# A ninth pair of quadrant products in a two-layer transformer block's second feed-forward

## The chip, the cores and the metric

The kernel runs on one core of one Trainium2 chip. The core has a matrix engine (TensorE, PE in the profile; its weight loads are PEld), a vector engine (VectorE, DVE), an activation engine (ScalarE, ACT), a general engine (GpSimd, POOL), a queue that issues transfers (SyncE, SP) and 16 DMA engines. The engines run their own instruction streams in order and meet at semaphores. Working memory is the SBUF of 128 partitions; TensorE writes to PSUM. The metric is the device time of one execution in microseconds (us), as the median of several runs.

## The reference, cut to what matters

One sequence of 512 tokens and 1024 features runs through two layers, in float32. Each layer mixes (spatial gating in the first, forgetting attention in the second, memory attention in both) and then runs a gated feed-forward of width 2816:

```python
f = rmsnorm(h, ln_ffn_pre[layer])
f = (jax.nn.silu(f @ w_ffn_gate[layer]) * (f @ w_ffn_up[layer])) @ w_ffn_down[layer]
h = h + rmsnorm(f, ln_ffn_post[layer])
```

The change is in the feed-forward of the second layer, whose output is the kernel's output.

## The kernel before, in words

**Numbers in two parts.** Each float32 operand is split into a high part (a cast on ScalarE, L276) and a low part (a subtraction on VectorE, L277). A product of two operands is three products on TensorE: high by high, high by low, low by high (`mm3`, L219 to L221). The split parts of a weight block, 128x512 each, go into `pair_of_parts` (L125), a ring of eight pairs.

**Row tiles.** The hidden width of 2816 is 22 row tiles of 128 rows, 0 to 21. For each row tile, gate and up are matrix products of weight blocks with the normed input; then the hidden value is silu(gate) times up. Row tiles 0 and 1 are computed plainly at the boundary from the mixing stage. The others come in pairs (2 and 3, 4 and 5, to 20 and 21).

**Seven products for eight.** For a pair of row tiles and the two halves of the input, `Seven` (L1098) takes a two-by-two block product with seven quadrant products in place of eight. `run(n)` does quadrant n: 12 products of 128x256 on TensorE, then evacuations on ScalarE and a sum on VectorE (L1150 to L1170). After the seventh (`run(3)`) the rows are handed on: `gate_rows` (L1309) applies the row scale and silu, `up_rows` (L1315) multiplies gate and up. A set (`sets(m)`, L1327) is one `Seven` for gate and one for up, for row tiles m and m+1; the last quadrant of each is run after the first two quadrants of the next, where there is a next.

**Down, in quadrants and plainly.** The down product of most pairs also goes by seven quadrant products (`Down`, L1174): the two row tiles by the two halves of the tokens and of the output. Its operands are sums of hidden values, formed on VectorE (`sums`, `last_sum`) and split (`form`); its weights are loaded and summed (`weights`), some sums by transfers that add in DRAM (`sums_ahead`, L170). A quadrant is six products of 128x512. One quadrant runs during the sets (`straight`, L1333). The other six wait until all sets are done: a first pass takes quadrants 0, 3, 6 and 5 of each pair, a second pass quadrants 1 and 4. Before the change `ones = 8` pairs go this way, row tiles 2 to 17.

**The tail.** The remaining row tiles, 18 to 21, are computed by two further sets after the passes; `up_rows` splits their hidden values at once (`some`). Their down product is done plainly in the tail (`tail_of`, L877), token tile by token tile (four of 128 tokens): for each of the two output halves, three products per row tile, so 24 products of 128x512 for a token tile; the last token tile's second half is done in two pieces of 256 columns. Then VectorE adds the product to the sum so far (L904), ScalarE squares it (L917), VectorE and GpSimd form the normalisation factor (L924, L290), and ScalarE scales the two halves (L944). `give` (L1708) turns them back on TensorE (L955), adds them to the residual on VectorE (L960) and sends them out; it does so for a token tile while the next one's products run. The last token tile has a variant of its own (L905 to L940, `give_last`).

**Places.** While the sets run, the residual rows are parked in DRAM and their tile, `room`, holds four places for weights of 128x1024; `more_raws` (L1298) hands them out in a circle: to the first gate set, to the up set's two loads from row tile 4 on, and in the passes to the weights of every second pair. `places` (L1303) makes a `Down` with its three tiles for hidden values and sums.

The order of the work on each engine comes from the code's order and a scheduler that may move an instruction ahead of others that wait; each engine then runs its stream in the order given.

Of the kernel before, what the change touches and what calls it, by code (L numbers as in the profile page):

```python
# [8 lines left out]
F32 = mybir.dt.float32  # L9
# [34 lines left out]
def hybrid(ctx: ExitStack, tc: tile.TileContext, i: dict, out: bass.AP):  # L44
# [14 lines left out]
    def name(s):  # L59
        n_of[s] = n_of.get(s, 0) + 1  # L60
        return f"{s}_{n_of[s]}"

    def act(s, dt=F32R, shape=(P, T)):
        return ap.tile(list(shape), dt, tag="a", name=name(s))

    def plain(s, shape=(P, T), dt=F32):
        return yp.tile(list(shape), dt, tag="y", name=name(s))
# [7 lines left out]
    def small(s, n=4, dt=F32):  # L75
        return sp.tile([P, n], dt, tag=f"s{n}", name=name(s))
# [131 lines left out]
    def down_weights(layer, k, dh, aside=False):  # L208
        return moving_pair(i["w_down"][layer, 4 * dh : 4 * dh + 4, :, k : k + 2, :]
                           .rearrange("m p k c -> p m (k c)"), aside)  # L210
# [145 lines left out]
    def rows_tile(s, dt=F32):  # L356
        return hp.tile([P, KT, T], dt, tag="h", name=name(s))
# [886 lines left out]
    def feed_forward(layer, phase, xp, meanwhile=None):  # L1244
        nonlocal h
        nnorm = PairNorm()
        rb = rbc
        ones = 8

        def hidden(gate, up, f, cols):  # L1250
            c0, c1 = cols
# [9 lines left out]
        fs = [(act("fhi"), act("flo")) for _ in range(2)]  # L1261
# [9 lines left out]
        a, close = boundary(phase, G_MIX_POST + layer, G_FFN_PRE + layer, nnorm, rb, first, evac_first, scaled)  # L1271
# [9 lines left out]
        xs, last = combined(a, scaled, xp)  # L1281
        last()
        ys = [[None] * 2 for _ in range(TB)]
# [9 lines left out]
                nc.sync.dma_start(kept_y[tb, dh], y)  # L1293

        room = rows_tile("room")
        places_of_raws = cycle([room[:, 2 * n : 2 * n + 2, :].rearrange("p a b -> p (a b)") for n in range(4)])

        def more_raws():  # L1298
            return next(places_of_raws)

        downs, gates = [], {}

        def places():  # L1303
            j = len(downs)
            downs.append(Down(layer, 2 + 2 * j, act("u", F32), plain("u"),
                              act("t", F32) if j < 4 else plain("t")))
            return downs[j].u0, downs[j].u1

        def gate_rows(row, g):  # L1309
# [16 lines left out]

        def sets(m, some=None):  # L1327
            sums_ahead()
            yield Seven(xs, "w_gate", layer, m, "mm", gate_rows, raws=more_raws if m == 4 else None)
            yield Seven(xs, "w_up", layer, m, "lg", lambda row, u: up_rows(row, u, some), None if some else places,  # L1330
                        more_raws if m > 2 else None)

# [32 lines left out]
        one, two, aside = [], [], []  # L1365
# [54 lines left out]
        for j, d in enumerate(downs):  # L1420
# [5 lines left out]
            if 0 < j < 7:  # L1426
                tb, dh, some = late[j - 1]
# [5 lines left out]
                    V.tensor_add(y, y, some)  # L1433
                    ys[tb][dh] = y

        fs = [(act("fhi"), act("flo")) for _ in range(4)]
        before = None
        for m in (18, 20):
            if meanwhile and m == 20:
                next(meanwhile)  # L1440
            for n, u in enumerate(sets(m, fs[m - 18 : m - 16])):
                u.run(1)
                u.run(7)
                if before:
                    before.run(3)
                for x in (6, 4, 5, 2) if n and m == 20 and not layer else (6, 4, 2, 5):
                    u.run(x)
                before = u
# [7 lines left out]
        eps = small("eps")  # L1456
        V.tensor_mul(eps, nnorm.r4, nnorm.r4)
        V.reciprocal(eps, eps)
        V.tensor_scalar_mul(eps, eps, RMS_EPS)
        return tail_of(fs, lambda kp, dh, aside: down_weights(layer, 18 + 2 * kp, dh, aside), ys, eps, layer == 1, True)  # L1460


    def layer_b(phase, fp):
# [237 lines left out]
    with tc.tile_pool(name="ffn0", bufs=4) as xp:  # L1701
        phase = feed_forward(0, phase, xp, memory())
    with tc.tile_pool(name="fox", bufs=1) as fp:
        phase = layer_b(phase, fp)
    with tc.tile_pool(name="ffn1", bufs=4) as xp:
        tail, ys, _ = feed_forward(1, phase, xp, end_gains())
# [102 lines left out]
```

## Time and profile before

| What | Value |
|---|---|
| Runs before: median, lowest, highest (3 runs) | 1083.52, 1082.90, 1083.83 us |
| Profiled execution: span | 1081.0 us |
| Runs' median less the span (what lies around it) | 2.5 us |
| TensorE busy | 1073.2 us, 99% of the span |
| VectorE busy | 942.9 us, 87% |
| ScalarE busy | 736.4 us, 68% |
| DMA, mean over the span | 166 GB/s |

The profile page gives no other time for the profiled execution than its span, from the first to the last instruction; what a run takes beyond it is the third row. In the views, a time is in us from the span's start. The chain of waits goes back from the last instruction, at each step to what released it. A group of instructions has a line, an engine, an operation, the names written and read with shapes, a count, the busy time and the mean length of one, then the idle time before it. In the order in time, a row is start, length, engine, line, operation, names, shapes, and in brackets the idle time just before and what ended it. Matmul records overlap: a record's length is more than the distance to the next one.

### The profile page before, as it was taken

Reading aid. Unit: us, or ns where it says so; the run is one execution under the profiler, and the core shown is the slowest. Engines: PE = TensorE matmul, PEld = TensorE weight load, DVE = VectorE, ACT = ScalarE, POOL = GpSimd, SP = SyncE. Lnnn points to the kernel's source line nnn. Section 1 sums busy time; section 2 is a strip of 40 time slices with the busy share of each in tenths; the row PEclk is TensorE's granted clock in tenths of the full one; section 3 lists DMA queues with packets and bytes.
Section 4 is the critical chain, followed back from the end, with each engine's and each line's share of the span. In section 5 each row is a group of like instructions: output and inputs, shape, how many; then the busy total and the mean of one; then the engine's idle time right before and its main releaser. Section 6 shows DMA issues by size and latency. Waiting matters only on the chain.

```text
span 1081.0 us, 20005 instructions
## 1 busy us (share of the span) xinstructions
PE 1073.2 (99%) x7234; PEld 982.1 (91%) x7234; DVE 942.9 (87%) x1894; ACT 736.4 (68%) x1605; POOL 74.4 (7%) x99
## 2 busy tenths in 40 slices
PE   9999999999999999999999999999999999999998
PEld 7998889999999988998988998889999999988996
DVE  8889659999989999996987899959999988999975
ACT  8776468666666667576765677858766666667564
POOL 0101001000000100000110111001000000000001
PEclk9999999999999999999999999999999999999999
DMA  7556666967665967264441754445977663646332
GB/s 275 167 136 180 190 157 204 255 186 194 172 169 149 300 177 230 92 206 126 128 128 48 208 128 115 126 123 171 255 199 194 162 158 115 176 128 206 112 118 79
DMA packets 131979, 179.52 MB, mean 166 GB/s; under 512 B 9964, under 2 KB 94200, under 8 KB 131880
## 3 DMA queue, kind: packets, MB, share of 16 engines
q1 hardware_dynamic: 119608, 160.53, 48.0%
q0 software_dynamic: 11712, 17.40, 10.3%
q8 instruction: 57, 0.93, 0.4%
q14 instruction: 42, 0.34, 0.1%
q10 hardware_dynamic: 560, 0.31, 0.1%
HBM read 158.71 MB, written 43.00 MB: 187 GB/s over the span
## 4 chain that ended last, share of the span: by engine, by line
PE 96%; ACT 2%; DVE 0%; issue 0%; DMA 0%; POOL 0%; POOLq 0%; ACTq 0%
PE a L219 7%; PE a L221 7%; PE a L220 7%; PE y L219 4%; PE y L220 4%; PE y L221 4%; PE ps L219 4%; PE ps L221 4%; PE ps L220 4%; PE e L219 4%; PE e L221 4%; PE e L220 3%; PE p L221 3%; PE p L219 3%; PE p L220 3%; PE x L219 3%
## 5 line engine op out<-in xcount | busy, mean ns | idle before, releaser
L276 ACT CAST whi<-raw 128x512 fp32r<-128x512 f32 x315 | 188.0, 618 | 59.8 <-PE a L220 12.9
L277 DVE TENSOR_TENSOR wlo<-raw,whi 128x512 fp32r<-128x512 f32 x315 | 210.2, 687 | 20.0 <-ACT whi L276 17.1
L219 PE MATMUL a<-xshi,whi 128*128 128x256 f32 x480 | 135.0, 281 | 0.0
L220 PE MATMUL a<-xslo,whi 128*128 128x256 f32 x480 | 134.9, 281 | 0.0
L221 PE MATMUL a<-xshi,wlo 128*128 128x256 f32 x480 | 134.7, 281 | 0.0
L276 ACT CAST whi<-room 128x512 fp32r<-128x512 f32 x160 | 98.1, 621 | 46.5 <-PE x L220 9.6
L277 DVE TENSOR_TENSOR wlo<-room,whi 128x512 fp32r<-128x512 f32 x160 | 108.9, 687 | 7.5 <-ACT whi L276 5.3
L219 PEld LDWEIGHTS a<-xshi,whi 128*128 128x128 f32 x480 | 90.3, 188 | 1.1 <-ACT e L1166 0.3
L220 PEld LDWEIGHTS a<-xslo,whi 128*128 128x128 f32 x480 | 90.4, 188 | 0.7
L221 PEld LDWEIGHTS a<-xshi,wlo 128*128 128x128 f32 x480 | 90.5, 189 | 0.0
L219 PE MATMUL ps<-xshi,whi 128*128 128x256 f32 x192 | 55.0, 289 | 0.1
L220 PE MATMUL ps<-xslo,whi 128*128 128x256 f32 x192 | 54.1, 283 | 0.0
L221 PE MATMUL ps<-xshi,wlo 128*128 128x256 f32 x192 | 54.0, 282 | 0.0
L276 ACT CAST ff<-u 128x256 fp32r<-128x256 f32 x80 | 32.3, 407 | 29.1 <-PE p L221 15.5
L219 PE MATMUL y<-whi,mixedhi 128*128 128x512 f32 x128 | 51.2, 400 | 0.0
L221 PE MATMUL p<-whi,ff 128*128 128x512 f32 x128 | 50.5, 395 | 0.0
L219 PE MATMUL p<-whi,ff 128*128 128x512 f32 x128 | 50.5, 395 | 0.0
L220 PE MATMUL y<-wlo,mixedhi 128*128 128x512 f32 x128 | 50.5, 395 | 0.0
L221 PE MATMUL y<-whi,mixedlo 128*128 128x512 f32 x128 | 50.4, 394 | 0.0
L220 PE MATMUL p<-wlo,ff 128*128 128x512 f32 x128 | 50.3, 393 | 0.0
L219 PE MATMUL x<-xshi,whi 128*128 128x256 f32 x160 | 45.1, 282 | 0.0
L220 PE MATMUL x<-xslo,whi 128*128 128x256 f32 x160 | 45.1, 282 | 0.0
(391 smaller groups left out, 3575.6 us busy)
## 6 DMA issues: line engine op xcount, KB each, us to landing
room<-in_w_up SPq DMA_DIRECT2D x36, 512.0 KB, 4.0
raw<-in_w_gate SPq DMA_DIRECT2D x24, 512.0 KB, 4.1
raw<-in_w_down SPq DMA_DIRECT2D x20, 512.0 KB, 4.5
sums<-in_w_gate SPq DMA_DIRECT2D x16, 512.0 KB, 5.8
sums<-in_w_gate POOLq DMA_DIRECT2D x16, 512.0 KB, 5.9
raw<-in_w_out SPq DMA_DIRECT2D x16, 512.0 KB, 3.5
sums<-in_w_down SPq DMA_DIRECT2D x32, 256.0 KB, 5.6
sums<-in_w_down POOLq DMA_DIRECT2D x16, 512.0 KB, 7.8
```

The costliest lines, as they stand in the source:

```text
L219: PE.matmul(o, w[0], x[0], start=start, stop=False, skip_group_check=more)
L220: PE.matmul(o, w[0], x[1], start=False, stop=False, skip_group_check=more)
L221: return PE.matmul(o, w[1], x[0], start=False, stop=stop, skip_group_check=more)
L276: last_hi[0] = A.copy(hi, src)
L277: last_split[0] = last_hi[0], (eng or V).tensor_sub(lo, src, hi)
```

## The change

In the second layer row tiles 18 and 19 join the quadrant products as a ninth pair, and the tail keeps row tiles 20 and 21. The two sets behind the passes become one; the other is run with the sets ahead of the passes. The ninth pair's three tiles for hidden values and sums lie in `room`, in rows 4 to 6, so `more_raws` has two places there in place of four; the first gate set alone uses the other two (`first_raws`). The first layer is unchanged.

```diff
-        ones = 8
+        ones = 9 if layer else 8
+        ends = (18, 20)[ones - 8 :]
...
-        places_of_raws = cycle([room[:, 2 * n : 2 * n + 2, :].rearrange("p a b -> p (a b)") for n in range(4)])
+        some_raws = [room[:, 2 * n : 2 * n + 2, :].rearrange("p a b -> p (a b)") for n in range(4)]
+        early_raws = iter(some_raws[2:])
+        places_of_raws = cycle(some_raws if ones == 8 else some_raws[:2])
...
+        def first_raws():
+            return more_raws() if ones == 8 else next(early_raws)
...
-            downs.append(Down(layer, 2 + 2 * j, act("u", F32), plain("u"),
-                              act("t", F32) if j < 4 else plain("t")))
+            three = (act("u", F32), plain("u"), act("t", F32) if j < 4 else plain("t")) if j < 8 else \
+                [room[:, n, :] for n in (4, 5, 6)]
+            downs.append(Down(layer, 2 + 2 * j, *three))
...
-            yield Seven(xs, "w_gate", layer, m, "mm", gate_rows, raws=more_raws if m == 4 else None)
+            yield Seven(xs, "w_gate", layer, m, "mm", gate_rows, raws=first_raws if m == 4 else None)
...
-        fs = [(act("fhi"), act("flo")) for _ in range(4)]
+        fs = [(act("fhi"), act("flo")) for _ in range(2 * len(ends))]
...
-        for m in (18, 20):
+        for m in ends:
...
-            for n, u in enumerate(sets(m, fs[m - 18 : m - 16])):
+            for n, u in enumerate(sets(m, fs[m - ends[0] : m - ends[0] + 2])):
...
-        return tail_of(fs, lambda kp, dh, aside: down_weights(layer, 18 + 2 * kp, dh, aside), ys, eps, layer == 1, True)
+        return tail_of(fs, lambda kp, dh, aside: down_weights(layer, ends[0] + 2 * kp, dh, aside), ys, eps, layer == 1, True)
```

The order of instructions shows two places. The first is TensorE's stream from the last quadrant product of the last up set (`a<-xshi`) into the tail (`y<-whi,fhi`). Before; here `fhi_13158` and `fhi_13160` are row tiles 18 and 19, `fhi_13162` and `fhi_13164` row tiles 20 and 21:

```order
L221 MATMUL a_13555<-xshi_9745,wlo_13689 128x256
L219 MATMUL y_13771<-whi_13737,fhi_13160 128x512
L220 MATMUL y_13771<-wlo_13738,fhi_13160 128x512 [waits DVE_49]
L221 MATMUL y_13771<-whi_13737,flo_13161 128x512
L219 MATMUL y_13807<-whi_13733,fhi_13158 128x512 [waits PE_49]
L220 MATMUL y_13807<-wlo_13734,fhi_13158 128x512
L221 MATMUL y_13807<-whi_13733,flo_13159 128x512
L219 MATMUL y_13807<-whi_13737,fhi_13160 128x512
L220 MATMUL y_13807<-wlo_13738,fhi_13160 128x512
L221 MATMUL y_13807<-whi_13737,flo_13161 128x512
L219 MATMUL y_13863<-whi_13733,fhi_13158 128x512
L220 MATMUL y_13863<-wlo_13734,fhi_13158 128x512
```

The next row of the stream before is the first that reads row tile 20 (`y_13771<-whi_13743,fhi_13162`, waiting for ScalarE). Three more products of row tile 18 stand between the last two quadrant products. Of the changed kernel, the same place; `fhi_13535` and `fhi_13537` are row tiles 20 and 21:

```order
L221 MATMUL a_13655<-xshi_9745,wlo_13789 128x256
L219 MATMUL y_13851<-whi_13833,fhi_13535 128x512 [waits Activation_49]
L220 MATMUL y_13851<-wlo_13834,fhi_13535 128x512 [waits DVE_49]
L219 MATMUL y_13875<-whi_13833,fhi_13535 128x512 [waits PE_49]
L219 MATMUL y_13861<-whi_13843,fhi_13535 128x512 [waits Activation_49]
L221 MATMUL y_13851<-whi_13833,flo_13536 128x512 [waits DVE_49]
```

The first tail product now follows the last quadrant product directly, and it reads a hidden value of that same set; the last two quadrant products follow each other directly too.

The second place is VectorE's stream in the tail of the changed kernel, from the residual of the first token tile (`yt_13899`, `yt_13909`) to the adds of the third (`y_13919`, `y_13929`):

```order
L904 TENSOR_TENSOR y_13469<-y_13885,y_13469 128x512 [waits PE_49]
L960 SCALAR_TENSOR_TENSOR h_13818<-yt_13899,gains,h_13818 128x128 [waits DMAHW6_49,PE_49]
L960 SCALAR_TENSOR_TENSOR h_13818<-yt_13899,gains,h_13818 128x128
L924 SCALAR_TENSOR_TENSOR v_13828<-ss_13827,eps_13823 128x1 [waits Activation_49]
L960 SCALAR_TENSOR_TENSOR h_13818<-yt_13899,gains,h_13818 128x128 [waits DMAHW7_49]
...
L904 TENSOR_TENSOR yb_13246<-y_13919,yb_13246 128x512 [waits PE_49]
L904 TENSOR_TENSOR y_13374<-y_13929,y_13374 128x512 [waits PE_49]
L960 SCALAR_TENSOR_TENSOR h_13818<-yt_13943,gains,h_13818 128x128 [waits PE_49]
```

Here the order is as before but for one row: the second token tile's L924 stands after two residual rows, where it stood after three. What is between the adds on TensorE is half of what it was.

## The prediction

> **What bounds the kernel now.** I read the page first, for the engines and the chain of waits.
>
> ```profile
> span 1081.0 us, 20005 instructions
> PE 96%; ACT 2%; DVE 0%; issue 0%; DMA 0%; POOL 0%; POOLq 0%; ACTq 0%
> ```
>
> TensorE carries 96% of the chain that ends last. An edit that takes products away therefore pays in full, as long as what is left still covers the waits. Next I read the windows by stage, in the second feed-forward only (columns: window, length, then busy time and count of PE, PEld, DVE, ACT, POOL, then clock, DMA share and GB/s).
>
> ```profile
> 943.00:988.00 45.00, 45.00 (x195) 36.38 (x194) 43.08 (x83) 31.30 (x69) 0.00 (x0) 1.00 0.47 133
> 1051.00:1069.00 18.00, 18.00 (x87) 14.51 (x86) 11.96 (x30) 10.06 (x23) 1.67 (x3) 1.00 0.12 33
> ```
>
> In the first pass over the quadrant products (943 to 988) TensorE never pauses, with VectorE close behind it. In the tail (1051 to 1069) TensorE never pauses either, and VectorE is busy 11.96 of 18 us: a third of its time is spare. The change halves TensorE's work in exactly that stretch, and leaves the work behind it. So two things have to be priced: the products, and the cover.
>
> **The products.** The group of the first pass's products, and two pieces of the chain that stand two weight pairs of the first pass apart:
>
> ```profile
> L219 PE MATMUL p<-whi,ff 128*128 128x512 f32 x64 | 25.3, 395 | 0.0
> ...
> 954.54 0.24 PE p L219
> ...
> 965.69 0.24 PE p L219
> ```
>
> The 395 ns are the mean length of overlapping records; what counts is the pitch. Between 954.54 and 965.69 lie 2 pairs x 4 quadrants x 6 products = 48 products: 11.15 / 48 = 0.232 us each. The tail loses two of its four row tiles: by the order of instructions 42 products of 128x512 and 12 of 128x256 (the last token tile's second half is done in two pieces). At 0.232 us and, from the seam's rows below, 0.117 us for the short ones, that is 9.75 + 1.4 = 11.15 us. The ninth pair adds 7 quadrants x 6 = 42 products of 128x512, 9.75 us. The gate and up products of row tiles 18 and 19 are the same in number. **Products alone: -1.4 us.**
>
> The ninth pair's own VectorE and ScalarE work (net 14 instructions more on the one, 8 on the other) costs nothing: it lies in the passes, where a pair takes TensorE 11.15 / 2 = 5.58 us and VectorE 43.08 / 45 of that, 5.3 us. Without that cover it would be 14 x 0.6, some 8 us.
>
> **The seam before the tail.** The tail's first sums need the last row tile's hidden values, and these come late. TensorE there:
>
> ```profile
> 1045.07 0.28 PE L219 MATMUL a<-xshi,whi 128*128 128x256 f32 x1
> ...
> 1046.36 0.28 PE L221 MATMUL a<-xshi,wlo 128*128 128x256 f32 x1
> ...
> 1047.16 0.31 PE L219 MATMUL a<-xshi,whi 128*128 128x256 f32 x1
> ...
> 1048.55 0.28 PE L221 MATMUL a<-xshi,wlo 128*128 128x256 f32 x1
> ...
> 1051.22 0.50 PE L219 MATMUL y<-whi,fhi 128*128 128x512 f32 x1
> ```
>
> The next-to-last quadrant product of the last up row starts its twelve products from 1045.07 to 1046.36, 0.117 us apart, and is through at 1046.48. The last quadrant product runs from 1047.16 to 1048.67 (its twelfth starts at 1048.55), 1.4 us at that pitch. The first tail product that needs the last row tiles starts at 1051.22. Into the two gaps the schedule has put tail products of row tiles 18 and 19: 3 in the first, 11 in the second, 14 x 0.232 = 3.25 us. What they wait for, on VectorE and ScalarE:
>
> ```profile
> 1047.07 0.69 DVE L1167 TENSOR_TENSOR s<-e,s 128x512 f32<-128x512 f32 x1 [3.33 <-ACT e L1166]
> 1047.79 0.69 DVE L1317 SCALAR_TENSOR_TENSOR s<-s,s 128x512 f32<-128x512 f32 x1
> 1049.23 0.69 DVE L277 TENSOR_TENSOR flo<-s,fhi 128x512 fp32r<-128x512 f32 x1 [0.74 <-ACT fhi L276]
> 1049.84 0.68 DVE L1321 TENSOR_TENSOR s<-s,s 128x512 f32<-128x512 f32 x1
> ...
> 1046.68 0.36 ACT L1166 COPY e<-a 128x256 f32<-128x256 f32 x1 [1.04 <-PE a L221]
> ...
> 1048.58 0.62 ACT L276 CAST fhi<-s 128x512 fp32r<-128x512 f32 x1 [1.54 <-DVE s L1317]
> ...
> 1050.55 0.62 ACT L276 CAST fhi<-s 128x512 fp32r<-128x512 f32 x1 [1.09 <-DVE s L1321]
> ```
>
> This is one dependent chain: copy at 1046.68, sum at 1047.07, product at 1047.79, cast at 1048.58, its low part at 1049.23, the other row's product at 1049.84, its cast from 1050.55 to 1051.17. From 1046.48 to 1051.22 it takes 4.74 us, whatever TensorE does. In the changed kernel the same instructions stand in the same order, but row tiles 18 and 19 are no longer in the tail, so nothing covers them: of the 4.74 us TensorE has work for 1.4 us and **idles for 3.3 us**. Seen from the start of the tail (call it t0, 1051.22 in this profile): t0 moves by the ninth pair's whole 9.75 us, since the 14 products that leave from ahead of t0 give nothing back.
>
> **The tail behind t0.** Before, from t0 to VectorE's last sum take 1073.34 - 1051.22 = 22.1 us (the row is below). Behind t0 28 long and 12 short products go, 6.5 + 1.4 = 7.9 us. Paced by TensorE the stretch would be 14.2 us. Whether VectorE and ScalarE keep that pace is worked out from these rows (L904 adds a product to its sum, L917 squares it, L924 and L290 make the factor, L944 scales both halves, L955 transposes, L960 adds to the residual):
>
> ```profile
> 1053.19 0.69 DVE L904 TENSOR_TENSOR ya<-y,ya 128x512 f32<-128x512 f32 x1
> 1057.76 0.21 DVE L924 SCALAR_TENSOR_TENSOR v<-ss,eps 128x1 f32<-128x1 f32 x1
> 1061.53 1.38 DVE L960 SCALAR_TENSOR_TENSOR h<-yt,gains,h 128x128 f32<-128x128 f32 x5
> 1071.40 0.42 DVE L904 TENSOR_TENSOR y<-y,y 128x256 f32<-128x256 f32 x1
> 1073.34 0.42 DVE L904 TENSOR_TENSOR y<-y,y 128x256 f32<-128x256 f32 x1
> ...
> 1053.92 0.63 ACT L917 ACTIVATE sq<-ya 128x512 bf16<-128x512 f32 x1 [0.66 <-DVE ya L904]
> 1054.46 0.19 ACT L917 ACTIVATION_READ_ACCUMULATOR sq<-ya 128x1 f32 x1
> 1058.66 0.72 ACT L944 ACTIVATE ya<-ya,r 128x512 f32<-128x512 f32 x1
> 1059.30 0.71 ACT L944 ACTIVATE y<-y,r 128x512 f32<-128x512 f32 x1
> ...
> 1058.06 0.57 POOL L290 TENSOR_TENSOR r<-v,mhalf 128x1 f32<-128x1 f32 x1 [187.49 <-DVE v L924]
> ...
> 1059.71 0.60 PE L955 MATMUL yt<-ident,ya 128*128 128x128 f32 x4
> ```
>
> In the changed order of each engine, in us after t0, an add holding VectorE 0.6, a residual 0.275 (1.38 / 5): the first token tile's two sums are added at 2.1 and 3.2, squared until 4.7; the third add holds VectorE, so L924 comes at 5.0, the power at 5.3, the two scalings from 5.9 to 7.2. Only then does ScalarE square the second tile's second half (to 7.9): L924 at 8.0, power until 8.85, scalings to 10.2. VectorE's eight residuals of the first tile run from 7.35 to 9.8, with the L924 among them, and in its order the third tile's adds stand behind them, 9.8 to 11.0, although TensorE had delivered at 8.2 and 9.6. Squares to 12.0, L924 at 12.05, power, scaling to 13.7, four transposes, and from 14.4 to 15.5 the first four residuals of the third tile; behind them stands the last tile's first short add, and the last follows 1.95 us later, as 1073.34 follows 1071.40: at 17.45. So the stretch is **17.45 us, not 14.2**: of the 7.9 us, 4.65 are kept. The end behind it (7.7 us, 1073.34 to 1081.0) is the same chain and stays.
>
> **Sum**: +9.75 - (22.1 - 17.45) = **+5.1 us** on the span; the same as -1.4 for products, +3.25 for the lost cover, +3.25 for the tail's own chain. The median of the runs, 1083.52, lies 2.5 us above the profiled span, and I carry that over: 1088.6 us.
>
> **The buffers.** The sets' up weights now have two places in the room tile, not four, so each set's load waits for the set before.
>
> ```profile
> 884.59 5.79 SPq L164 DMA_DIRECT2D room<-in_w_up  x2
> ...
> 889.33 0.69 DVE L277 TENSOR_TENSOR wlo<-room,whi 128x512 fp32r<-128x512 f32 x1
> ...
> 874.63 0.62 ACT L276 CAST whi<-room 128x512 fp32r<-128x512 f32 x1 [0.61 <-PE x L221]
> ...
> 895.92 0.62 ACT L276 CAST whi<-room 128x512 fp32r<-128x512 f32 x1 [0.61 <-PE x L221]
> ...
> 884.36 0.28 PE L219 MATMUL a<-xshi,whi 128*128 128x256 f32 x1
> ...
> DMA to landing us min/median/max: 3.4/3.8/4.1
> ...
> DMA to landing us min/median/max: 3.4/4.1/9.3
> ```
>
> The last read of a set's first place ends at 890.02, where SP's second load goes out; the next set's first cast is at 895.92, and its product 9.7 us after the cast (884.36 after 874.63). So a load has 5.9 us and takes at most 4.1 (the upper of the two landing rows, for this tile from 815 to 900): hidden, with 1.8 us spare, and 8.4 us of finished splits behind that. I take 0.
>
> **Rivals.** (a) *The tail keeps TensorE's pace*: squares and scalings overlap better than the order reads. For it: VectorE's spare third; against it: residuals and adds in one queue. +9.75 - 7.9 = +1.8 us: 1085.4. (b) *Nothing waits at the seam*, the other side: if the last tile's values were there before TensorE is through, the product count alone would decide, -1.4 us: 1082.1, not slower. It decides from a chain of 1.4 us instead of 4.74, and every row of the chain waits for the row before it, so I see little for it. (c) *The sets starve*: the slowest load issued by L164 in the whole run took 9.3 us (the lower landing row); seven sets each 3.4 us late are 24 us, less the lead of 8.4: +15 on top, 1104. Against it are the 4.1 us above. (d) *TensorE's clock falls in the gap.*
>
> ```profile
> 1079.50:1080.00 0.50, 0.00 (x0) 0.00 (x0) 0.00 (x0) 0.00 (x0) 0.00 (x0) 0.62 0.11 29
> 1075.63 1.09 PE L955 MATMUL yt<-ident,yg 128*128 128x128 f32 x8 [1.08 <-ACT yg L1728]
> 1.25 3.66 PE L88 MATMUL idle<-idle 128*128 128x512 bf16 x9 [1.25 <-DVE idle L85]
> ```
>
> At the kernel's end the mean granted clock of this half microsecond is 0.62, as from a fall from 1.0 to 0.5 at 1079.6, 2.9 us after the last transposes end (1076.72); the seam's longer gap is 2.6 us. The nine products that open the program took 0.407 us each. At that rate the first 12 products behind t0 (2.8 us) take 4.9: +2.1 on top, 1090.7. [...]
>
> **Chances.** The sum 0.62 (its own range 1087.0 to 1090.2), (a) 0.14, (b) 0.06, (c) 0.05, (d) 0.13. Range 1085.2 to 1091.4: below it lie (b) and a part of (a), above it (c) and a part of (d). A measurement of this kernel tells about 0.2%, 2.2 us, from no change: slower by more than that are the sum, (c), (d) and a third of (a), 0.84; within it the rest of (a) and half of (b), 0.13; faster the other half of (b), 0.03.
>
> **What would show it.** Right: about 3.3 us of idle TensorE between the last up product and the tail, ended by the cast of the last hidden values; in the tail TensorE waiting for L944 and VectorE running L960 and L904 without pause; 16.5 to 18.5 us from t0 to the last add; the passes as dense as now. Wrong: idle TensorE inside the nine sets (c), a tail of about 14 us (a), no gap at the seam (b), or long products behind t0 (d).

## The result, and the profile after

The changed kernel takes 1088.17 us (median of 5 runs, 1087.68 to 1089.82) against 1082.9 us before (5 runs, 1082.63 to 1083.83): a ratio of 1.0050, 95% interval 1.0039 to 1.0062, so 4.2 to 6.7 us slower. The forecast was 1088.6, worked out as 5.1 us on top of 1083.52; between the two medians here it is 5.3. A second set of five runs, reported below, gave a median of 1089.23 and a ratio of 1.0057 (1.0045 to 1.0070).

The page of the changed kernel, its profiled execution (timed at 1089.82 us, the longest of the five):

```profile
span 1088.0 us, 20025 instructions
PE 92%; ACT 3%; DMA 1%; DVE 1%; issue 1%; POOL 1%; POOLq 0%; ACTq 0%
```

TensorE's share of the chain fell from 96 to 92%: the chain now leaves TensorE in some places. Not all of the 7.0 us between the spans comes from the change. The last power that GpSimd forms for a norm ahead of the second feed-forward is work that both kernels do alike; first before, then after:

```profile
753.91 1.07 POOL L290 TENSOR_TENSOR r<-var,mhalf 128x2 f32<-128x2 f32 x1 [5.13 <-DVE var L320]
```

```profile
755.26 1.07 POOL L290 TENSOR_TENSOR r<-var,mhalf 128x2 f32<-128x2 f32 x1 [5.13 <-DVE var L320]
```

This execution was 1.35 us late before it reached any changed instruction. From this mark to the end it is 327.1 us before and 332.7 after: **+5.65 us**. In what follows, lengths of single executions are taken from this mark.

**The sets** run without a stall; each marker in them is late by the same 1.35 us. **The first pass** has one new gap. TensorE, then ScalarE, in order of time:

```profile
960.81 0.39 PE L221 MATMUL x<-whi,ff 128*128 128x512 f32 x1
961.57 0.38 PE L219 MATMUL a<-xshi,whi 128*128 128x256 f32 x1 [0.38 <-ACT e L1166]
...
958.00 0.62 ACT L276 CAST whi<-room 128x512 fp32r<-128x512 f32 x1 [0.74 <-DMA room<-in_w_down]
...
961.15 0.36 ACT L1166 COPY e<-a 128x256 f32<-128x256 f32 x1
```

At the pitch of 0.232 us the next product was due at 961.04; it starts at 961.57, so 0.53 us are lost. It waits for an evacuation on ScalarE at 961.15, and that one comes late: ScalarE stood 0.74 us for weights that land in the room tile (958.00), and the casts behind stand ahead of the evacuation.

**The seam**, TensorE, and the cast on ScalarE that ends it:

```profile
1058.80 0.39 PE L219 MATMUL a<-xshi,whi 128*128 128x256 f32 x1 [0.45 <-ACT e L1166]
...
1060.21 0.28 PE L221 MATMUL a<-xshi,wlo 128*128 128x256 f32 x1
1062.94 0.50 PE L219 MATMUL y<-whi,fhi 128*128 128x512 f32 x1 [2.45 <-ACT fhi L276]
...
1062.27 0.62 ACT L276 CAST fhi<-s 128x512 fp32r<-128x512 f32 x1 [1.09 <-DVE s L1328]
```

Two gaps, 0.60 us ahead of the last quadrant product and 2.61 behind it, where the kernel before had the products of row tiles 18 and 19: 3.2 us. t0, the first product that needs the last hidden values, is at 1062.94.

**The tail.** Seventeen microseconds of it in the view by windows (columns as in the prediction), then TensorE's last product and VectorE's rows in order of time:

```profile
1063.00:1080.00 17.00, 15.68 (x90) 12.99 (x90) 13.98 (x40) 10.22 (x24) 2.95 (x4) 1.00 0.28 77
```

```profile
1076.22 0.28 PE L221 MATMUL y<-whi,flo 128*128 128x256 f32 x1
...
1071.05 1.64 DVE L960 SCALAR_TENSOR_TENSOR h<-yt,gains,h 128x128 f32<-128x128 f32 x6
1072.60 0.68 DVE L904 TENSOR_TENSOR yb<-y,yb 128x512 f32<-128x512 f32 x1
1073.20 0.68 DVE L904 TENSOR_TENSOR y<-y,y 128x512 f32<-128x512 f32 x1
1073.80 0.86 DVE L960 SCALAR_TENSOR_TENSOR h<-yt,gains,h 128x128 f32<-128x128 f32 x3
...
1076.12 0.68 DVE L904 TENSOR_TENSOR yb<-y,yb 128x512 f32<-128x512 f32 x1
1077.09 1.13 DVE L960 SCALAR_TENSOR_TENSOR h<-yt,gains,h 128x128 f32<-128x128 f32 x4 [0.29 <-PE yt L955]
...
1080.04 0.41 DVE L904 TENSOR_TENSOR y<-y,y 128x256 f32<-128x256 f32 x1
```

VectorE was busy 11.96 of 18 us in the tail before; now it is 13.98 of 17, and from 1071.05 on residuals (L960) and sums (L904) stand back to back, but for 0.29 us ahead of 1077.09 and a few short rows. From t0 to the last sum it is 1080.04 - 1062.94 = 17.10 us. TensorE itself shows no wait in this stretch: its last product starts at 1076.22, 13.3 us after t0, and the last sum comes 3.8 us behind it.

**The end.** The filling transposes and the last eight transposes, TensorE:

```profile
1077.65 1.04 PE L915 MATMUL idle<-ident 128*128 128x128 f32 x8
1082.32 1.97 PE L955 MATMUL yt<-ident,yg 128*128 128x128 f32 x8 [3.63 <-ACT yg L1735]
```

The eight took 1.09 us before, behind a wait of 1.08. Now they come after 3.63 us without a product and take 1.97: the granted clock had fallen to 0.50 at about 1081.6, ahead of them (a mean of 0.58 from 1081.5 to 1082.0, 0.50 from there on). From the last sum to the end it is 1088.0 - 1080.04 = 7.96 us, where it was 7.66.

### The profile page after: what moved, and what is told of

It is laid out like the page before. It is cut to its first block, busy times and chain, and to the rows that moved or that the text cites. A ratio compares the mean times of both kernels' runs of the same rounds, so it can differ in the third digit from the quotient of the medians.

```text
span 1088.0 us, 20025 instructions
## 1 busy us (share of the span) xinstructions
PE 1074.8 (99%) x7222; PEld 982.1 (90%) x7222; DVE 948.8 (87%) x1908; ACT 739.8 (68%) x1613; POOL 76.9 (7%) x100
## 4 chain that ended last, share of the span: by engine, by line
PE 92%; ACT 3%; DMA 1%; DVE 1%; issue 1%; POOL 1%; POOLq 0%; ACTq 0%
PE a L219 7%; PE a L220 7%; PE a L221 7%; PE y L219 4%; PE y L220 4%; PE y L221 4%; PE e L219 3%; PE e L221 3%; PE e L220 3%; PE ps L219 3%; PE ps L221 3%; PE ps L220 3%; PE p L221 3%; PE p L219 3%; PE p L220 3%; PE x L219 3%
## 5 line engine op out<-in xcount | busy, mean ns | idle before, releaser
L277 DVE TENSOR_TENSOR wlo<-raw,whi 128x512 fp32r<-128x512 f32 x316 | 210.7, 685 | 20.3 <-ACT whi L276 17.1
L219 PE MATMUL p<-whi,ff 128*128 128x512 f32 x136 | 53.7, 395 | 0.0
L221 PE MATMUL p<-whi,ff 128*128 128x512 f32 x136 | 53.7, 395 | 0.0
L220 PE MATMUL p<-wlo,ff 128*128 128x512 f32 x136 | 53.5, 393 | 0.0
L276 ACT CAST ff<-u 128x256 fp32r<-128x256 f32 x80 | 32.3, 406 | 28.1 <-PE p L221 15.4
```

The costliest lines, as they stand in the source:

```text
L219: PE.matmul(o, w[0], x[0], start=start, stop=False, skip_group_check=more)
L220: PE.matmul(o, w[0], x[1], start=False, stop=False, skip_group_check=more)
L221: return PE.matmul(o, w[1], x[0], start=False, stop=stop, skip_group_check=more)
L276: last_hi[0] = A.copy(hi, src)
L277: last_split[0] = last_hi[0], (eng or V).tensor_sub(lo, src, hi)
```

## The experiments

They ran in three sets, each beside the kernel before: the uncovered kernel, the two places, the kernel without residuals and the held products (median of the kernel before 1083.54 us there); the two kernels with the seam filled, with and without residuals, the other room and the shared residuals (1083.55); the changed kernel again, the two tiles shared and all mended (1083.02). "Length" is from the mark on GpSimd to the end of the span in the profiled execution, "t0" from the mark to the first product that needs the last hidden values, "t0 to end" what is left. The runs of one kernel spread over 0.6 to 4.3 us, and the marks alone lie between 753.7 and 756.1, so lengths tell small effects better than medians do.

| Kernel | Median (us) | Ratio to before, 95% | Length | t0 | t0 to end |
|---|---|---|---|---|---|
| before | 1082.9 | 1 | 327.1 | 297.3 | 29.8 |
| changed | 1088.17 | 1.0039 to 1.0062 | 332.7 | 307.7 | 25.1 |
| changed, again | 1089.23 | 1.0045 to 1.0070 | 332.2 | 307.1 | 25.1 |
| before, seam uncovered | 1087.46 | 1.0025 to 1.0050 | 330.2 | 297.3 | 32.9 |
| before, two places | 1083.63 | 0.9993 to 1.0010 | 327.5 | 297.7 | 29.8 |
| changed, no residuals | 1088.49 | 1.0034 to 1.0059 | 332.4 | 307.7 | 24.7 |
| changed, products held | 1086.21 | 1.0019 to 1.0037 | 330.7 | 305.7 | 25.0 |
| changed, seam filled | 1088.79 | 1.0039 to 1.0065 | 332.0 | 307.2 | 24.8 |
| seam filled, no residuals | 1087.37 | 1.0022 to 1.0049 | 330.5 | 307.3 | 23.2 |
| changed, other room | 1088.67 | 1.0038 to 1.0063 | 332.1 | 307.0 | 25.1 |
| changed, residuals shared | 1089.78 | 1.0045 to 1.0070 | 333.8 | 307.2 | 26.6 |
| seam filled, two tiles shared | 1088.07 | 1.0036 to 1.0061 | 332.6 | 308.0 | 24.7 |
| changed, all mended | 1087.18 | 1.0023 to 1.0051 | 330.4 | 304.8 | 25.6 |

### The lost cover, alone, in the kernel before

Only the order of the row tiles in the last tail is changed; the products are as many as before. (Row tiles 20 and 21 are summed first, so nothing else is ready at the seam.)

```diff
-                for k in range(nk):
+                some = (2, 3, 0, 1) if last else range(nk)
+                for k in some:
                     w = [part[:, m0:m1, :] for part in ws[k // 2, dh][k % 2]]
-                    token_products(o[:, cols], xs[k], w, tb, k == 0, k == nk - 1)
+                    token_products(o[:, cols], xs[k], w, tb, k == some[0], k == some[-1])
```

> The kernel before, with one edit: in the last tail each sum takes row tiles 20 and 21 first and 18 and 19 behind them, so no tail product can run before the last set's hidden values are there. Same products, same results but for the order of addition. Theory (the cover at the seam is worth what it held): the 14 products that filled the seam move behind t0, TensorE idles 3.2 to 3.3 us in two gaps of 0.6 and 2.6 us, and the tail of four row tiles still runs at TensorE's pace, so +3.2 us, about 1086.1. Rival (the tail has slack that takes the gap up, as with three tails' worth of VectorE time spare): less than +1 us.

Measured: 1087.46 us, 3.9 above the kernel before (2.7 to 5.4 by the interval). TensorE's wait at the seam, and VectorE's last sum:

```profile
1051.51 0.50 PE L219 MATMUL y<-whi,fhi 128*128 128x512 f32 x1 [2.45 <-ACT fhi L276]
...
1076.74 0.41 DVE L905 TENSOR_TENSOR y<-y,y 128x256 f32<-128x256 f32 x1
```

t0 is where it was (297.3 from the mark), and the 14 products that stood ahead of it now lie behind: 25.23 us to the last sum, where it was 22.12. The length grew by 330.2 - 327.1 = 3.1 us. So the cover at the seam is worth what its products take, in a tail that TensorE paces.

### The two places in the room tile, alone

The kernel before with only the change of buffers.

```diff
-        places_of_raws = cycle([room[:, 2 * n : 2 * n + 2, :].rearrange("p a b -> p (a b)") for n in range(4)])
+        some_raws = [room[:, 2 * n : 2 * n + 2, :].rearrange("p a b -> p (a b)") for n in range(4)]
+        early_raws = iter(some_raws[2:])
+        places_of_raws = cycle(some_raws[:2] if layer else some_raws)
...
-            yield Seven(xs, "w_gate", layer, m, "mm", gate_rows, raws=more_raws if m == 4 else None)
+            yield Seven(xs, "w_gate", layer, m, "mm", gate_rows, raws=first_raws if m == 4 else None)
```

> The kernel before with the buffer change alone: up weights of the second layer have two places in the room tile in place of four, the first gate set the other two; eight pairs and a tail of four row tiles as before. Theory (loads are hidden in the sets; only the first pass's second pair comes late): a stall of 0 to 0.6 us near the first pass, 1083.0 to 1083.5. Rival (sets starve): +3 us or more.

Measured: 1083.63 against 1083.54 us, a ratio of 1.0002 (0.9993 to 1.0010). The medians show no cost. The profile shows a small one, in the first pass, at the place of the changed kernel's gap (ScalarE, then TensorE):

```profile
935.36 0.62 ACT L276 CAST whi<-room 128x512 fp32r<-128x512 f32 x1 [0.46 <-DMA room<-in_w_down]
...
938.41 0.40 PE L221 MATMUL x<-whi,ff 128*128 128x512 f32 x1
938.93 0.39 PE L219 MATMUL a<-xshi,whi 128*128 128x256 f32 x1
```

At 0.232 us the product was due at 938.64, so 0.29 us are lost, and t0 comes 0.4 us later (297.7 against 297.3). The kernel before has neither the wait nor the gap there. So the change of buffers alone can make the new gap.

### The tail without VectorE's residuals

The residual sums of the first three token tiles are left out (the outputs of these tokens lack it); the transposes and all the rest stay.

```diff
-        for x, k in enumerate(some):
-            residual(tr[:, x * P : (x + 1) * P], k, (c.start, c.stop), G_FFN_POST + 1)
```

> The changed kernel without the residual adds of the first three token tiles (24 of VectorE's 128x128 instructions; the output of those tokens is then not the reference's). Theory (VectorE's queue paces the tail from the first residual on): 24 x 0.275 = 6.6 us of its work go, t0 to the last add falls from 17.1 to about 14.1 us and TensorE is the pace: -3.0 us, about 1085.2. Rival (the chain of square, factor and scaling from token tile to token tile sets the pace): under 1 us less, since that chain is untouched.

Leaving the sums out does one thing more: the transfers out of these token tiles wait for nothing then, and go at 1058.8 to 1062.6, where the changed kernel sends them at 1071.7 to 1080.1.

Measured: 1088.49 us, no gain. But two things met in its profile. The view by windows behind t0 (1062.54; the clock is the number ahead of the DMA share):

```profile
1063.00:1064.00 1.00, 1.00 (x6) 0.81 (x5) 1.00 (x3) 0.54 (x2) 0.00 (x0) 1.00 1.06 285
1064.00:1065.00 1.00, 1.00 (x4) 0.73 (x4) 0.42 (x1) 0.00 (x0) 0.00 (x0) 0.50 1.07 294
...
1066.00:1067.00 1.00, 1.00 (x3) 0.79 (x3) 0.00 (x0) 0.63 (x2) 0.00 (x0) 0.50 0.00 0
1067.00:1068.00 1.00, 1.00 (x5) 0.77 (x4) 0.69 (x1) 0.00 (x0) 0.00 (x0) 0.80 0.00 0
```

The granted clock fell to 0.50 at about 1064.0, 1.5 us behind the end of the gap, and came back at 1067.4 (a mean of 0.80 in the last window is 0.4 us at half). Eight products in there stand 0.43 us apart, not 0.232. This is rival (d), which the profile of the changed kernel (1.00 in the window of its tail, above) does not show. So this run could not tell the theory from its rival, and the next two were made to separate them.

### The seam filled with products that nobody reads

```diff
+        fill = ps("tr", s="idle") if layer else None
+        def filler(some):
+            for x in range(some if layer else 0):
+                w = xs[0][0][0]
+                PE.matmul(fill[:, :256], w[:, :P], w[:, :256], start=True, stop=True)
+        filler(5)
         before.run(3)
+        filler(21)
```

> The changed kernel with 26 products of 128x256 whose sums nobody reads, put into the two gaps at the seam (5 ahead of the last quadrant product, 21 behind it: 0.6 and 2.5 us at 0.117 us each). They need nothing but operands that are long there, so TensorE no longer idles, but no useful work is moved. If idling in itself costs nothing and only the late hidden values do (my theory), the time stays at that of the changed kernel, 1088.2 (within 0.6), the last tiles' first product starts where it did, and from it to VectorE's last sum it is again about 17.1 us. If the granted clock falls behind the gap in a part of the executions, as it did in the profiled one of the kernel without residuals (nine products at 0.43 us, some 1.7 us), the filled kernel is faster by up to that: 1086.5 to 1087.5. If the filling products were in the way, 1088.5 to 1089.

Measured: 1088.79 us. TensorE at the seam and at the end:

```profile
1058.67 2.68 PE L1461 MATMUL idle<-xshi 128*128 128x256 f32 x21
1061.29 0.50 PE L219 MATMUL y<-whi,fhi 128*128 128x512 f32 x1
...
1080.68 1.09 PE L955 MATMUL yt<-ident,yg 128*128 128x128 f32 x8 [3.63 <-ACT yg L1744]
```

TensorE does not idle at the seam at all, t0 comes no sooner (307.2 from the mark; the changed kernel has 307.7 with the gap at 961 and 307.1 without), and from t0 to the last sum (1078.40) it is 17.11 us against 17.10. So at this seam idling in itself costs nothing; the late values do. The median shows no gain either. Nor is the fall of the clock what makes the changed kernel slower: its own two profiles show no fall in the tail (the clock at 1.00 from 1063 to 1080 in the first, the products behind the gap 0.23 us apart in the second), and are 5.65 and 5.1 us longer all the same.

### Without residuals, with the seam filled

The two edits above together.

> The filled kernel without the residual sums of the first three token tiles (their outputs are then not the reference's). It separates the two things that met in the kernel without residuals. VectorE's queue (theory): with the clock kept, the stretch from the last tiles' first product to the last sum falls from 17.1 us to between 14.2 (TensorE's pace) and 15.2 (16.9 as measured without residuals, less 1.7 for the nine slow products); 1085.3 to 1086.3 us. Rival, the chain of squares, power and scaling alone sets the tail: the stretch stays at 16.5 to 17.1, and the time at 1087.6 to 1088.2.

Measured: 1087.37 us, between what the theory and the rival gave. The view by windows of the tail, and in it VectorE's waits and TensorE's:

```profile
1061.60:1077.00 15.40, 14.93 (x82) 11.94 (x82) 8.32 (x17) 10.18 (x24) 2.96 (x4) 1.00 0.20 56
```

```profile
1069.62 0.22 DVE L924 SCALAR_TENSOR_TENSOR v<-ss,eps 128x1 f32<-128x1 f32 x1 [1.41 <-ACT sq L917]
...
1073.12 0.22 DVE L924 SCALAR_TENSOR_TENSOR v<-ss,eps 128x1 f32<-128x1 f32 x1 [1.02 <-ACT sq L917]
...
1076.98 0.42 DVE L904 TENSOR_TENSOR y<-y,y 128x256 f32<-128x256 f32 x1
...
1074.78 0.66 PE L955 MATMUL yt<-ident,yb 128*128 128x128 f32 x4 [0.46 <-ACT yb L944]
```

The clock stays at 1.00, and from t0 (1061.64) to the last sum it is 15.34 us. Against 17.11 that is 1.77 us for the residuals on VectorE; against 16.88 in the run above it is 1.54 us for the fall of the clock, which is 8 x (0.425 - 0.232). With VectorE busy only 8.32 of 15.4 us the tail still is 1.1 us longer than TensorE's 14.2: the chain that it waits for now runs through ScalarE. VectorE's L924 stands 1.41 and 1.02 us for squares, and the scaling behind it holds TensorE's transposes (1074.78), which stand ahead of the last short products. So both the theory and its rival hold a part: 1.8 us go with VectorE's residuals, and 1.1 stay. That the 1.1 are the chain of squares, power and scaling is read from these rows; no run took that chain away.

### Half of the residuals taken from VectorE

ScalarE multiplies the second half's transposed blocks by their gains, GpSimd adds them.

```diff
-        for x, k in enumerate(some):
-            residual(tr[:, x * P : (x + 1) * P], k, (c.start, c.stop), G_FFN_POST + 1)
+        if some[0]:
+            t = temp("gv", (P, 4, P))
+            for x, k in enumerate(some):
+                A.activation(t[:, x, :], tr[:, x * P : (x + 1) * P], AF.Copy, scale=gain(G_FFN_POST + 1, k))
+            G.tensor_tensor(out=h[:, 4:8, c], in0=t, in1=h[:, 4:8, c], op=ALU.add)
+        else:
+            for x, k in enumerate(some):
+                residual(tr[:, x * P : (x + 1) * P], k, (c.start, c.stop), G_FFN_POST + 1)
```

> The changed kernel, with the second half of the residual sums of the first three token tiles taken from VectorE: ScalarE multiplies the four transposed blocks by their gains on the way out of PSUM and GpSimd adds them to the residual in one instruction. VectorE loses 12 x 0.275 = 3.3 us in the tail. Theory (VectorE's queue of sums and residuals sets the tail): 1 to 3 us faster than the changed kernel, 1085.2 to 1087.2. Rival: ScalarE, which gets 12 more instructions between its squares and scalings, becomes the bound: 1088 to 1090.

Measured: 1089.78 us, no gain and rather a loss. Two mishaps are in its profile. The clock, in windows around its t0 (1062.35), and GpSimd's last rows:

```profile
1062.00:1063.00 1.00, 0.65 (x2) 0.57 (x3) 0.67 (x2) 1.00 (x3) 0.00 (x0) 0.82 0.00 0
1063.00:1064.00 1.00, 1.00 (x3) 0.72 (x3) 1.00 (x3) 0.34 (x1) 0.00 (x0) 0.50 0.03 8
...
1066.00:1067.00 1.00, 1.00 (x5) 0.80 (x5) 0.64 (x1) 0.33 (x1) 0.00 (x0) 0.98 0.00 0
```

```profile
1080.73 1.26 POOL L1726 TENSOR_TENSOR h<-gv,h 128x512 f32<-128x512 f32 x1 [0.75 <-ACT gv L1725]
1081.95 0.55 POOL L290 TENSOR_TENSOR r<-v,mhalf 128x1 f32<-128x1 f32 x1
```

The clock fell here too, from about 1062.64 (0.82 on the mean is 0.36 us at half) to 1066.04. And the last power, whose operand was there at 1080.87, stood 1.1 us behind GpSimd's last sum. Both hide what the edit did. The product ahead of the first transposes came 7.92 us after t0 (1070.27), against 6.37 in the changed kernel (1069.31), so the fall took some 1.55 us, and still the last sum came 17.24 us after t0, about as in the changed kernel. Without the fall it would be some 15.7 us, an estimate; so the twelve moved sums may well have won about 1.4 us, which the late power lost again (9.31 us from the last sum to the end, where it was 7.96). No run has them with the seam filled. The next one has eight:

### Two token tiles shared, seam filled

The same edit for the first two token tiles only (`if some[0] and tb < TB - 2`), with the seam filled.

> The changed kernel with the seam filled by unread products, and with the second half of the residual sums of the first two token tiles only (8 of 24) taken over by ScalarE and GpSimd; the third tile's stay on VectorE, so that GpSimd is free for the last power. Theory (VectorE's queue holds 1.77 of the tail's 17.1 us, the difference to the filled kernel without any residual): the stretch falls to 15.9 to 16.5 us, the time to 1087.0 (1086.6 to 1087.8). Rival, ScalarE's squares and scalings are as full: the stretch stays at 17 us, 1088.2 to 1088.8.

Measured: 1088.07 us. From t0 (1063.65) to the last sum (1080.52) it is 16.87 us, 0.24 less than without the edit and far from the 15.9 to 16.5 that VectorE's queue alone would give. The tail by windows:

```profile
1064.00:1081.00 17.00, 15.94 (x90) 12.54 (x88) 13.06 (x34) 11.84 (x32) 5.51 (x6) 1.00 0.19 53
```

VectorE has 0.9 us less, ScalarE 1.6 more than in the changed kernel, and TensorE now waits for ScalarE's scaling ahead of its last products:

```profile
1077.29 0.66 PE L955 MATMUL yt<-ident,yb 128*128 128x128 f32 x4 [0.32 <-ACT yb L944]
```

The rival is nearer: with eight sums moved, the wait is handed on to ScalarE.

### Products held back for the seam

Of the last two pairs, the six products each of one quadrant of the second pass are held until the seam: three ahead of the last quadrant product, nine behind it.

```diff
             for n in (1, 4):
+                if layer and n == 4 and j >= ones - 2:
+                    hold(d, j == ones - 1)
+                    continue
                 d.product(n, o[n], j == 0, j == ones - 1)
...
+        for x in held[:1]:
+            mm3(*x)
         before.run(3)
+        for x in held[1:]:
+            mm3(*x)
+        if held:
+            tap(4)
```

> The changed kernel with 12 products of the second pass (quadrant 4 of the last two pairs) held back to the seam, their operands split where they were before and kept. Theory (TensorE idles 3.2 us at the seam): 10 of the 12 stand in the two gaps by the order, 2.3 us of idling goes, while VectorE gets two adds of 0.6 us in the tail: -1.1 to -2.3 us, about 1086.4. Rival (the tail's chain, not TensorE, sets the end, and t0 does not depend on it): no change within 0.5 us, since t0 stays where the last hidden value is; it only moves if the work in front of it gets shorter.

Measured: 1086.21 us, 2.0 below the changed kernel. TensorE and the last transposes:

```profile
1061.78 0.50 PE L219 MATMUL y<-whi,fhi 128*128 128x512 f32 x1 [0.84 <-ACT fhi L276]
...
1081.39 1.09 PE L955 MATMUL yt<-ident,yg 128*128 128x128 f32 x8 [3.63 <-ACT yg L1756]
```

The wait fell from 2.45 to 0.84 us and t0 came 2.0 us sooner (305.7 from the mark), although this execution has 0.76 us of the gap in the first pass, where the changed kernel's had 0.53. The stretch behind it did not shrink (17.33). A cover of real work gives back what filling with unread products did not: the term of the seam, tried from the other side.

### Another place for the second pair's weights

```diff
-                downs[j].weights(1, more_raws if j % 2 else None)
+                downs[j].weights(1, more_raws if j % 2 and not (layer and j == 1) else None)
```

> The changed kernel, with the second weight pair of the first pass loaded into the ring that the even pairs use, not into the room tile's place that the last up set frees late. Theory: the new gap of 0.53 us in the first pass (TensorE waits there for an evacuation that stands behind the cast of these weights) goes, everything behind it comes 0.5 us sooner: 1087.7 against 1088.2, and no gap over 0.15 us between the last up set and the seam in the profile. Rival: the ring's own place comes as late, or the gap is made by something else: 1088.2 and the gap stays.

Measured: 1088.67 us. TensorE at the place of the gap:

```profile
960.30 0.40 PE L221 MATMUL x<-whi,ff 128*128 128x512 f32 x1
960.54 0.28 PE L219 MATMUL a<-xshi,whi 128*128 128x256 f32 x1
```

The gap is gone and t0 is 0.7 us sooner from the mark, but the median does not show it. The next run explains a part of that.

### The changed kernel once more

> The changed kernel itself once more, beside the two kernels below and with a profile of its own. Median 1088.2 within 0.7. In its profile: 2.6 us without a product at the seam; the stretch from the last tiles' first product to VectorE's last sum 17.1 us if the products behind the gap stay 0.23 us apart, about 18.6 if some of them stand 0.43 apart (the fall cost 1.54 us in the kernel without residuals: 16.88 against 15.34 with the gap filled); and a gap of anything between 0 and 0.8 us in the first pass near 961 us, as the five profiles with the room tile's place showed.

Measured: 1089.23 us, 1.0 above the 1088.2 expected and outside the 0.7 given. In its profile the gap in the first pass is absent, ScalarE's cast having waited less for the same transfer; the seam and the end are as before:

```profile
955.91 0.62 ACT L276 CAST whi<-room 128x512 fp32r<-128x512 f32 x1 [0.18 <-DMA room<-in_w_down]
```

```profile
1060.85 0.50 PE L219 MATMUL y<-whi,fhi 128*128 128x512 f32 x1 [2.46 <-ACT fhi L276]
```

17.09 us from t0 to the last sum, the products behind the gap 0.23 us apart, 7.96 to the end. Of the eight profiled executions of the changed kernel and its variants that load these weights into the room tile, five have the gap (0.19, 0.53, 0.58, 0.76 and 0.84 us) and three have none, or at most 0.1: it goes with when a transfer lands (ScalarE stood 0.74 us for it in the first profile, 0.18 in the second), and is worth 0.4 us on the mean.

### All mended

The held products, the other place for the weights, the two shared token tiles, and 36 filling transposes (L915) where there were 8.

> The changed kernel with four things mended: twelve products of the second pass held for the seam (measured alone: 2.0 us), the second pair's weights in the even ring (0.3, a part of the gap near 961), 28 more filling transposes ahead of the last eight (0.3, when the clock has fallen there), and 8 residual sums shared out (1.2 by the theory of VectorE's queue). Sum: 1088.2 - 3.8 = 1084.4 (1083.6 to 1085.4), faster than the changed kernel but not than the one before. Rival: the held products and the shared residuals act on the same wait, and only one of them counts: 1085.3 to 1086.2.

Measured: 1087.18 us, 1.0 below the changed kernel's first median (2.0 below its second, in the same set), but not below the one with held products alone, and above what both the sum and the rival gave. GpSimd, then VectorE, around the last sum (1073.29):

```profile
1071.80 1.28 POOL L919 TENSOR_TENSOR yg<-yb,gr 128x512 f32<-128x512 f32 x1
1073.04 0.73 POOL L290 TENSOR_TENSOR r<-v,mhalf 128x1 f32<-128x1 f32 x1
...
1073.29 0.41 DVE L904 TENSOR_TENSOR y<-y,y 128x256 f32<-128x256 f32 x1
...
1075.28 1.13 DVE L960 SCALAR_TENSOR_TENSOR h<-yt,gains,h 128x128 f32<-128x128 f32 x4 [1.12 <-PE yt L955]
1076.32 0.21 DVE L921 SCALAR_TENSOR_TENSOR two<-ss,eps 128x1 f32<-128x1 f32 x1
1076.45 1.12 DVE L960 SCALAR_TENSOR_TENSOR h<-yt,gains,h 128x128 f32<-128x128 f32 x4
1077.48 0.48 DVE L908 CUSTOM_DVE_ANT_0 sq<-y,two 128x256 bf16<-128x256 f32 x1
```

t0 came 2.9 us sooner than in the changed kernel (304.8 from the mark), and the last sum only 14.25 us behind it (1059.04 to 1073.29). But this is in part a matter of order: the third token tile's eight residuals, which stood ahead of the last sum in the changed kernel, now stand behind it (1075.28, 1076.45). They come late because that tile's power stood on GpSimd until 1073.04, although its operand was there at 1071.85: GpSimd had another product of the tail to do, behind a shared sum. VectorE's last step (L908, 1077.48) waits behind the residuals, and from the last sum to the end it is 11.3 us, where it was 7.96. What the tail won, the end lost; the length, 330.4, is that of the held products alone (330.7). No kernel of these beats the one before.

## Why the prediction was right, point by point

**Products, -1.4, and the seam, +3.25.** t0 moved by 10.37 us from the mark, 9.81 in the execution without the gap at 961; 9.75 was forecast. The idle time is 3.2 us, ended by the cast of the last hidden values. Uncovering the seam in the kernel before cost 3.1 us by itself, covering it in the changed one with real products gave 2.0 back (1.5 by the length against the changed kernel's second profile), covering it with unread ones gave nothing. The -1.4 was not tried alone; it is a part of these sums. The three seams speak for the dependent chain as the cause, against TensorE's idling as such and against rival (b).

**The tail, +3.25.** From t0 to the last sum 17.10 us, forecast 17.45 (TensorE's pace 14.2, rival a). The size was right and the chain that was read from the order is there, but its reasons are now told apart: 1.8 us of the 2.9 over TensorE's pace go when VectorE's residuals go, and 1.1 stay, which the rows put on ScalarE's chain. The forecast's steps had both, and they came nearly as worked out: the first residual 7.5 us after t0 (7.35 was forecast), the third tile's adds from 9.7 (9.8), its residuals from 14.2 (14.4). Of its two signs, "VectorE running without pause" was seen; "TensorE waiting for L944" was not: TensorE ran ahead, and VectorE's sums came late behind it. That sign appears when residuals are taken from VectorE (0.46 and 0.32 us), and faintly with the products held (0.16).

**The buffers, 0.** Right for the sets, which was where it was worked out: no stall there, and the change of places alone made 0.1 us between medians, with 0.29 us of a gap in its profile. What the step missed is the first pass, where the second pair's weights go to one of the same two places and land late for ScalarE: 0 to 0.84 us, 0.53 in the first profile. The estimate looked at each set's load and not at the next user of the same place.

**The end, "the same".** 7.96 us where 7.66 was carried over: the last eight transposes ran for 1.97 us, not 1.09. Behind 3.63 us without a product the eight ran with the clock at 0.50, 0.88 us longer than before; but the last transfer went out 3.3 us before the end of the span, where it was 3.8 before, so that only 0.3 is left. It is not so in each execution: after the same 3.63 us the transposes took 1.09 in the kernel with held products and in the filled one.

**What lies around the span.** 2.5 us were carried over as median less profiled span. The changed kernel's profiled execution took 1089.82 - 1088.0 = 1.8 us more than its span, and every run whose span is on record 1.7 to 1.8. So what lies around the span is not 2.5 us: the other 0.7 came from an execution profiled at the low end of its runs. It did not hurt the forecast of a median, since the change is added to a median: the sum worked out, 5.1, stands beside 5.65 (5.1 without the gap) in the two profiles of the changed kernel and 5.3 between the medians. That the sum came so near is in part luck: against the forecast, the first profile has t0 0.62 us later (0.53 of it the gap that was put at nothing), the stretch behind it 0.35 shorter and the end 0.30 longer.

**Rivals.** (c) is excluded by the run with two places; (b) by the seam's rows; (a) would need 14.2 us in the tail, where 17.1 were measured. (d) did happen, in two of the profiled executions of kernels whose seam stays empty, the ones without residuals and with shared residuals. It cost 1.54 us where 2.1 was forecast (eight slow products, not twelve). How often it happens in unprofiled runs is open. Filling the seam did not lower the median, but the intervals of the two kernels (1.0039 to 1.0065 and 1.0039 to 1.0062) would hide a share of about 1 us.

## What to carry to other kernels

Before work is moved out of a tail, ask what it covers there: the fourteen products that looked like TensorE's own cost were also what ran while the last row tile's values were finished. A tail of half the matrix work did not take half the time here, where the vector work stayed (17.10 us from t0 to the last sum, where it was 22.12); read the engine that will be next, in its order of instructions, and then the one after it, since moving eight of VectorE's sums to ScalarE and GpSimd gave 0.24 us. A single profile is one draw: compare lengths from a mark that both kernels share, not whole spans.

## What the runs showed of the hardware

The granted clock fell to 0.50 behind a gap of 2.6 us, 1.5 us after products had begun again in one execution (without residuals) and 0.3 us after it in another (residuals shared). Behind the same gap it stayed at 1.00 in the first profile of the changed kernel, and in its second, in the kernel with the other room and in the uncovered kernel before the products stand 0.23 us apart, as they do at 1.00. So it fell in two of six profiled executions in which gaps of 0.6 and 2.6 us stand 1.4 us apart; what decides it, no run shows. The slow stretch was 3.4 us long in both (1064.0 to 1067.4 and 1062.64 to 1066.04). At the end of the program the clock fell 2.9 us after the filling transposes in the changed kernel (1078.7 to 1081.6), ahead of the last eight, which took 1.97 us; in the kernel with held products the last eight began 3.63 us after the end of the filling transposes (1077.8 to 1081.4) and took 1.09.
